# Where the encoder memory is split in a hybrid encoder step, and which engines square it

## The chip, the cores and the metric

One core of one Trainium2 chip. The time is device microseconds for one execution of the whole program; lower is better. The engines are TensorE (PE; its weight loads are listed apart as PEld), VectorE (DVE), ScalarE (ACT), GpSimd (POOL) and SyncE (SP), which issues the DMAs of the weights.

## The reference

One inference step of a two-layer streaming encoder with width 1024, for a prompt of 256 frames and a sample group of 32 frames that share the weights. Layer 0 has two attentions side by side, A (chunk-band attention with a position bias) and B (forgetting attention, whose bias is a running sum of log gates), eight heads of 64 each, with normalised queries and keys. Layer 1 has C (stick-breaking attention). Each layer then has cross-attention into 256 memory tokens, and an MLP with a squared ReLU. The parts that matter here:

```python
def rmsnorm(x, g):
    xf = x.astype(jnp.float32)
    y = xf * lax.rsqrt(jnp.mean(xf * xf, axis=-1, keepdims=True) + EPS)
    return (y * g.astype(jnp.float32)).astype(x.dtype)

def mem_kv(mem, g_mem, w_kv, k_gain):
    b, n, _ = mem.shape
    k, v = jnp.split(rmsnorm(mem, g_mem) @ w_kv, 2, axis=-1)
    k = rmsnorm(k.reshape(b, n, N_HEADS_X, HEAD_DIM_X), k_gain)
    return k, v.reshape(b, n, N_HEADS_X, HEAD_DIM_X)
```

The memory is the same in both layers, so the mean of its squares is computed once, in layer 0.

## The kernel before

All activations lie feature-major: 8 tiles of 128 features by 288 frames (256 + 32), the memory 8 tiles of 128 by 256. Products in full precision are three matmuls: every operand is split into a rounded high part and a low rest (`wh`, `wl` for weights, `xh`, `xl`, `mh`, `ml` and so on), and lines 159 to 161 (in `mm3`, called by `gemm`) multiply high by high, low by high and high by low. A projection of one chunk of 256 weight columns is two output tiles of 128 columns, eight feature tiles each, three matmuls, so 48 matmuls, into two of three PSUM banks (`ps_g`). Scaling by the factor of the input norm comes after the projection, when a bank is emptied: `t` (line 407) for queries and keys of A and B, `vT` (line 431) for values, `tmk` (line 353) for the memory's keys, which needs `memrs`, the factor from the memory's squares.

Weights stream in half chunks of four feature tiles (512 KB) through `load_chunk`: SP issues the load into one of four buffers of the ring `raw`, ACT rounds it to `wh` (line 144), and DVE, or every few times POOL, subtracts to get `wl` (line 145), in a ring of three half chunks.

The head norm (`headnorm`, `sum_parts`, called by `project_qk`) takes five buffers for each of two output tiles from the ring `f`, which has eight: `t`, its square `sqh`, the two parts `sh` and `sl` of that for a matmul against a block of ones, and the factor `r`.

`mem_split` loads the memory in two DMAs of 512 KB into the ring `raw` as well (`mraw`), makes `mh` on ACT and `ml` on DVE (tiles of the ring `sp`, which has four: `oh` and `ol` of the attention outputs take the others), and in layer 0 also the sum over the eight feature tiles of the squares: the first square goes directly into `mssum`, each of the seven others into a buffer `sqm` of the ring `f`, and is then added. `mem_rms` multiplies the sum by ones on PE and makes `memrs`.

The order of the program in layer 0 is written by hand in `ORD_AB`: `qA0` projects queries and keys of A's first four heads, `pA0` their values, `aA0` attends, `F` makes the forget gates, `M` is `mem_split`, `N` is `mem_rms` (its matmuls tied behind the last projection matmul traced before it), `K0` to `K3` project the memory's keys. A scheduler then lays out each engine's queue from this program order and the buffers that are free, so work of neighbouring steps is interleaved. B's attention needs its bias, which POOL builds at lines 845 and 846; the bias tiles `b1`, `b0` and `bsmp` have two buffers each.

Of the kernel before, what the change touches and what calls it, by code (L numbers as in the profile page):

```python
# [10 lines left out]
AF = mybir.ActivationFunctionType  # L11
ALU = mybir.AluOpType
# [3 lines left out]
NP_ = 256  # L16
# [13 lines left out]
HPG = 0  # L30
VT2 = 1
SHE = 0
ORD_AB = 'qA0 pA0 F qA1 pA1 aA0 M qB0 aA1 qB1 pB0 pB1 aB0 N K2 aB1 K0 K3 K1'.split()
ORD_C = 'M q0 q1 p0 a0 q2 p1 a1 q3 p2 a2 p3 a3 K0 K1 K2 K3'.split()
ORD_X = 's1 s2 s3 s0 v0 v1 S v2 v3'.split()
NWARM = 9
# [16 lines left out]
def body(ctx: ExitStack, tc: tile.TileContext, i: dict, o: dict):  # L53
    nc = tc.nc
    mm = nc.tensor.matmul
    dve = nc.vector
    act = nc.scalar.activation
# [237 lines left out]
    def mem_split(layer):  # L295
        mh = spp.tile([P, KT, T], F32R, tag="sp", name="mh")
        ml = spp.tile([P, KT, T], F32R, tag="sp", name="ml")
        if layer == 0:
            ssum = scr.tile([P, T], F32, tag="ssum", name="mssum", bufs=2)
        for k in range(KT):  # L300
            if k % 4 == 0:
                raw = wraw.tile([P, 4, NP_], F32, tag="raw", name="mraw")
                nc.sync.dma_start(out=raw, in_=i["memT"][:, k:k + 4, :])
            m = raw[:, k % 4, :]
            g = gT[:, 3, layer, k:k + 1]
            act(mh[:, k, 0:NP_], m, AF.Copy, scale=g)
            dve.scalar_tensor_tensor(ml[:, k, 0:NP_], m, g, mh[:, k, 0:NP_].bitcast(F32), ALU.mult, ALU.subtract)  # L307
            if layer == 0:
                if k == 0:
                    nc.gpsimd.tensor_tensor(ssum[:, 0:NP_], m, m, ALU.mult)  # L310
                else:
                    sq = scr.tile([P, T], F32, tag="f", bufs=FB, name="sqm")
                    nc.gpsimd.tensor_tensor(sq[:, 0:NP_], m, m, ALU.mult)
                    nc.gpsimd.tensor_tensor(ssum[:, 0:NP_], ssum[:, 0:NP_], sq[:, 0:NP_], ALU.add)
        return mh, ml, ssum if layer == 0 else None

    def mem_rms(ssum):
# [541 lines left out]
    qk, vs, mk0 = {}, {}, {}  # L859
    for step in ORD_AB:  # L860
        op, at = step[0], step[1:]
        kind, g = ("AB".index(at[0]), int(at[1])) if len(at) == 2 else (0, 0)
        if op == "q":
            qk[at] = project_ab(kind, g)
        elif op == "p":
            vs[at] = values_ab(kind, g)
        elif op == "a":
            group_ab(kind, g, *qk[at], vs[at])
        elif op == "F":
            forget()  # L870
        elif op == "M":
            mh, ml, msum = mem_split(0)
        elif op == "N":

            with tc.issue_after(last_mm[0].ins):
                mem_rms(msum)
        else:
            R.after = last_mm[0].ins if at == "0" else R.after
            mk0[int(at)] = mem_k(0, int(at), mh, ml)
# [15 lines left out]
    for step in ORD_C:  # L895
        op, g = step[0], int(step[1:] or 0)
        if op == "q":
            qk[g] = project_qk("sb_w", g, 4 + g, xh, xl, rs, None, "ckT", g)
        elif op == "p":
            vs[g] = project_v("sb_w", 8 + g, xh, xl, rs, "cvT", g)  # L900
        elif op == "a":
            attend_c(g, *qk[g], vs[g], *caches("cckT", "ccv", g), oh, ol)
        elif op == "M":
            mh, ml, _ = mem_split(1)
        else:
            mk1[g] = mem_k(1, g, mh, ml)
# [115 lines left out]
```

## Time and profile before

| | us |
|---|---|
| median of 3 runs (lowest to highest) | 976.09 (975.94 to 976.49) |
| the profiled execution | 975.05 |
| its span, first to last instruction | 973.4 |
| PE busy in the span | 956.0 |
| DVE busy | 682.8 |
| ACT busy | 542.8 |
| POOL busy | 251.4 |

The mean granted clock of TensorE is 0.996 of full speed. Layer 0's mixer, with the steps of `ORD_AB`, takes about the first 180 us, and the memory's split lies between 38 us (its loads) and 86 us. Rows of the profile name the engine, the line and the tiles, with buffer numbers left out; L144 is line 144 of the kernel. Times in the rows are microseconds from the start of the span; means are in nanoseconds.

### The profile page before, as it was taken

The page shows a single profiled execution, that of the slowest core. Times are in us where ns is not written, and L with a number is a line of the kernel's source. Part 1 is how long each engine was busy: PE and PEld are TensorE (multiplying, and loading weights), DVE is VectorE, ACT ScalarE, POOL GpSimd, SP SyncE. Part 2 cuts the span into 40 slices and gives each one's busy share as a digit, 9 for nine tenths or more (in the row PEclk, how much of TensorE's full clock was granted, in tenths as well). Part 3 has the DMA queues.
Part 4 walks back from the last instruction along what each step waited for, and adds up shares of the span by engine and source line. Part 5 has one row for each costly group of instructions (what it writes and reads, how often), then busy time and mean ns, then how long its engine had stood idle before and what let it go on. Part 6 is the DMA issues. An engine that isn't in the chain of part 4 may idle for free.

```text
span 973.4 us, 19368 instructions
## 1 busy us (share of the span) xinstructions
PE 956.0 (98%) x7276; PEld 922.0 (95%) x7276; DVE 682.8 (70%) x1460; ACT 542.8 (56%) x1268; POOL 251.4 (26%) x291
## 2 busy tenths in 40 slices
PE   8997999999999999999999999999999999999998
PEld 7996798899999999999999999989999999999998
DVE  7787777769778766777695666678987766564643
ACT  6665577555546644445474767765544555354531
POOL 5335322221112212121112332234443211111210
PEclk9998999999999999999999999999999999999999
DMA  8654343554455545555465444356444455555452
GB/s 264 235 171 140 132 166 118 197 185 154 153 172 174 168 159 170 164 164 169 158 214 193 134 150 146 118 174 207 152 145 136 154 173 166 162 167 169 162 172 73
DMA packets 50702, 160.03 MB, mean 164 GB/s; under 512 B 6296, under 2 KB 12968, under 8 KB 50352
## 3 DMA queue, kind: packets, MB, share of 16 engines
q1 hardware_dynamic: 46864, 148.69, 47.5%
q0 software_dynamic: 2592, 8.92, 2.4%
q10 hardware_dynamic: 1152, 1.18, 0.4%
q8 instruction: 57, 0.93, 0.4%
q14 instruction: 37, 0.30, 0.1%
HBM read 148.65 MB, written 10.12 MB: 163 GB/s over the span
## 4 chain that ended last, share of the span: by engine, by line
PE 95%; DVE 3%; DMA 1%; ACT 1%; issue 1%; SPq 0%; DVEq 0%
PE g L159 28%; PE g L161 27%; PE g L160 27%; PE po L474 1%; DVE wl L145 1%; PE za L474 1%; PE za L579 1%; PE s L517 1%; DVE ml L307 1%; DMA raw<-in_ab_w_dram 0%; PE zs L619 0%; DMA h<-in_xT_dram 0%; PE sx L159 0%; PE za L600 0%; PE sx L161 0%
## 5 line engine op out<-in xcount | busy, mean ns | idle before, releaser
L144 ACT ACTIVATE wh<-raw 128x512 fp32r<-128x512 f32 (+3 forms) x561 | 279.8, 550 | 235.2 <-PE g L160 117.9
L145 DVE TENSOR_TENSOR wl<-raw,wh 128x512 fp32r<-128x512 f32 (+3 forms) x483 | 307.9, 671 | 116.0 <-ACT wh L144 109.8
L145 POOL TENSOR_TENSOR wl<-raw,wh 128x512 fp32r<-128x512 f32 (+2 forms) x141 | 175.2, 1243 | 520.1 <-ACT wh L144 423.9
L159 PE MATMUL g<-xh,wh 128*128 128x288 f32 (+1 forms) x1032 | 302.9, 298 | 2.5 <-DVE t L407 1.5
L160 PE MATMUL g<-xl,wh 128*128 128x288 f32 (+1 forms) x1032 | 303.9, 297 | 1.0 <-DVE xl L197 1.0
L161 PE MATMUL g<-xh,wl 128*128 128x288 f32 (+1 forms) x1032 | 302.2, 297 | 1.3 <-DVE wl L145 1.3
L159 PEld LDWEIGHTS g<-xh,wh 128*128 128x128 f32 (+1 forms) x1032 | 192.3, 188 | 5.0 <-DVE t L407 2.1
L161 PEld LDWEIGHTS g<-xh,wl 128*128 128x128 f32 (+1 forms) x1032 | 192.8, 188 | 3.3 <-DVE wl L145 2.2
L160 PEld LDWEIGHTS g<-xl,wh 128*128 128x128 f32 (+1 forms) x1032 | 193.3, 188 | 2.7 <-DVE xl L197 1.7
L160 PE MATMUL g<-hl,wh 128*128 128x288 f32 x512 | 150.3, 295 | 0.0
L159 PE MATMUL g<-hh,wh 128*128 128x288 f32 x512 | 148.9, 295 | 0.0
L161 PE MATMUL g<-hh,wl 128*128 128x288 f32 x512 | 148.5, 294 | 0.0
L160 PEld LDWEIGHTS g<-hl,wh 128*128 128x128 f32 x512 | 96.1, 188 | 0.0
L161 PEld LDWEIGHTS g<-hh,wl 128*128 128x128 f32 x512 | 95.7, 188 | 0.0
L159 PEld LDWEIGHTS g<-hh,wh 128*128 128x128 f32 x512 | 95.3, 187 | 0.0
L160 PE MATMUL g<-ol,wh 128*128 128x288 f32 x256 | 75.1, 296 | 0.1
L159 PE MATMUL g<-oh,wh 128*128 128x288 f32 x256 | 73.9, 296 | 0.8 <-ACT oh L493 0.8
L161 PE MATMUL g<-oh,wl 128*128 128x288 f32 x256 | 73.5, 295 | 0.0
L775 DVE TENSOR_TENSOR h<-h,g 128x288 f32<-128x288 f32 x64 | 28.8, 450 | 29.6 <-PE g L161 29.5
L159 PEld LDWEIGHTS g<-oh,wh 128*128 128x128 f32 x256 | 47.4, 188 | 1.4 <-ACT oh L493 1.0
L160 PEld LDWEIGHTS g<-ol,wh 128*128 128x128 f32 x256 | 48.1, 188 | 0.3 <-DVE ol L494 0.3
L161 PEld LDWEIGHTS g<-oh,wl 128*128 128x128 f32 x256 | 47.6, 188 | 0.4 <-issue 0.4
(313 smaller groups left out, 1514.2 us busy)
## 6 DMA issues: line engine op xcount, KB each, us to landing
raw<-in_w_up_dram SPq DMA_DIRECT2D x64, 512.0 KB, 3.8
raw<-in_w_down_dram SPq DMA_DIRECT2D x64, 512.0 KB, 3.8
raw<-in_w_kv_dram SPq DMA_DIRECT2D x32, 512.0 KB, 3.8
raw<-in_sb_w_dram SPq DMA_DIRECT2D x24, 512.0 KB, 4.2
raw<-in_ab_w_dram SPq DMA_DIRECT2D x22, 512.0 KB, 4.4
raw<-in_w_q_dram SPq DMA_DIRECT2D x16, 512.0 KB, 4.2
raw<-in_w_o_dram SPq DMA_DIRECT2D x16, 512.0 KB, 4.0
raw<-in_ab_wo_dram SPq DMA_DIRECT2D x8, 512.0 KB, 3.8
```

What stands on the lines that cost most here:

```text
L144: act(wh[:, r, :], src, AF.Copy)
L145: e.tensor_tensor(wl[:, r, :], src, wh[:, r, :].bitcast(F32), ALU.subtract)
L159: mm(out, lh, rh, start=first, stop=False)
L160: mm(out, lh, rl, start=False, stop=False)
L161: return mm(out, ll, rh, start=False, stop=last)
L307: dve.scalar_tensor_tensor(ml[:, k, 0:NP_], m, g, mh[:, k, 0:NP_].bitcast(F32), ALU.mult, ALU.subtract)
L474: mm(po[64 * par:64 * par + 64, kk * P:NP_], vt[:, kk, cols], pts[par][kk], start=kk == 0, stop=kk == 1)
L517: mm(s[:, 0:NP_], q[:, P:NP_], kT[:, p, 0:NP_], start=True, stop=True)
L579: mm(za2, x[:, 0:P], y, start=f_, stop=False, skip_group_check=True)
L775: dve.tensor_tensor(h[:, kt, :], h[:, kt, :], ps[:, 0:T], ALU.add)
```

## The change

Two things. In `ORD_AB` the step `M` moves from behind `aA0`, ahead of `qB0`, to behind `qB1`, ahead of `pB0`. And the squares of the memory go from POOL to ACT, and the seven additions from POOL to DVE.

```diff
-ORD_AB = 'qA0 pA0 F qA1 pA1 aA0 M qB0 aA1 qB1 pB0 pB1 aB0 N K2 aB1 K0 K3 K1'.split()
+ORD_AB = 'qA0 pA0 F qA1 pA1 aA0 qB0 aA1 qB1 M pB0 pB1 aB0 N K2 aB1 K0 K3 K1'.split()
...
             if layer == 0:
                 if k == 0:
-                    nc.gpsimd.tensor_tensor(ssum[:, 0:NP_], m, m, ALU.mult)
+                    act(ssum[:, 0:NP_], m, AF.Square)
                 else:
                     sq = scr.tile([P, T], F32, tag="f", bufs=FB, name="sqm")
-                    nc.gpsimd.tensor_tensor(sq[:, 0:NP_], m, m, ALU.mult)
-                    nc.gpsimd.tensor_tensor(ssum[:, 0:NP_], ssum[:, 0:NP_], sq[:, 0:NP_], ALU.add)
+                    act(sq[:, 0:NP_], m, AF.Square)
+                    dve.tensor_tensor(ssum[:, 0:NP_], ssum[:, 0:NP_], sq[:, 0:NP_], ALU.add)
```

The title given to the change also names the sum tied behind the last projection and bias tiles twice; both stand in the kernel before already, and the diff does not touch them.

## The prediction

> **What bounds the kernel now.** I read the page first, then busy time by stretches, then what TensorE waited for, then the timelines of the one stretch that stands out.
>
> ```profile
> span 973.4 us, 19368 instructions
> PE 956.0 (98%) x7276; PEld 922.0 (95%) x7276; DVE 682.8 (70%) x1460; ACT 542.8 (56%) x1268; POOL 251.4 (26%) x291
> PE   8997999999999999999999999999999999999998
> PEclk9998999999999999999999999999999999999999
> PE 95%; DVE 3%; DMA 1%; ACT 1%; issue 1%; SPq 0%; DVEq 0%
> ```
>
> TensorE (PE) is the bound: 95% of the chain that ended last is its own work, and only 973.4 − 956.0 = 17.4 us of the span is idle. A change that touches no matmul can win only part of that, and of what a lowered clock costs. Both lie in one place, the fourth slice (73 to 97 us). By stretches (length; then busy time of PE, weight load, DVE, ACT, POOL, each with its count; granted clock, DMA share, GB/s):
>
> ```profile
> 30.00:75.00 45.00, 45.00 (x337) 42.34 (x336) 35.73 (x94) 29.14 (x77) 17.97 (x21) 1.00 0.57 181
> 75.00:90.20 15.20, 9.91 (x73) 7.18 (x73) 14.26 (x42) 9.74 (x27) 10.29 (x11) 0.92 0.51 159
> 90.20:140.00 49.80, 48.08 (x350) 43.65 (x349) 35.56 (x97) 30.58 (x84) 15.13 (x16) 0.96 0.40 133
> 180.00:190.00 10.00, 9.05 (x83) 8.35 (x82) 7.27 (x17) 6.80 (x17) 0.92 (x2) 1.00 0.68 235
> 190.00:973.00 783.00, 778.33 (x5970) 762.02 (x5969) 537.46 (x1066) 422.20 (x955) 186.01 (x199) 1.00 0.50 161
> ...
> 75.50:90.20 14.70, 0.34 (x2) 0.19 (x1) 0.92 0.52 161
> 90.20:94.60 4.40, 2.61 (x6) 1.99 (x6) 0.50 0.29 102
> ```
>
> Between 75.0 and 90.2 PE idles 15.20 − 9.91 = 5.29 us while DVE is busy 14.26 of 15.20: for these 15 us VectorE is the bound. The last two rows count line 160 alone, a third of each projection: two matmuls in 14.7 us, so PE lived on small attention products. Then, from 90.20 to 94.60, the clock is 0.50, which costs half of 4.40 = 2.2 us. The rest of the idle time is thin: 1.72 in 90 to 140, 0.95 in 180 to 190, 4.67 after that.
>
> Why the projections stood still shows in the timelines of DVE, ACT and POOL (start, length, engine, line, output<-input):
>
> ```profile
> 42.49 0.82 POOL L310 TENSOR_TENSOR mssum<-mraw 128x256 f32<-128x256 f32 x1
> ...
> 66.02 1.35 POOL L145 TENSOR_TENSOR wl<-raw,wh 128x512 fp32r<-128x512 f32 x1 [6.35 <-PE g L160]
> 66.10 0.50 ACT L183 ACTIVATE r<-ps_hn,epsb 128x288 f32<-128x288 f32 x1 [0.22 <-PE ps_hn L332]
> 67.33 4.71 POOL L313 TENSOR_TENSOR sqm<-mraw 128x256 f32<-128x256 f32 x6
> 68.18 0.44 DVE L407 TENSOR_TENSOR t<-g,rs 128x288 f32<-128x288 f32 x1
> 72.01 0.74 POOL L314 TENSOR_TENSOR mssum<-mssum,sqm 128x256 f32<-128x256 f32 x1
> 72.78 0.44 ACT L384 ACTIVATE sqh<-t 128x288 f32<-128x288 f32 x1 [1.67 <-POOL mssum L314]
> 74.97 0.38 ACT L488 ACTIVATE oh<-po 128x256 fp32r<-128x256 f32 x1 [0.71 <-PE po L474]
> 75.84 3.29 ACT L306 ACTIVATE mh<-mraw,gT 128x256 fp32r<-128x256 f32 x8
> 78.05 2.06 POOL L845 TENSOR_TENSOR b<-b,cq 128x1024 f32<-128x1024 f32 x1
> 78.28 2.00 DVE L328 CAST sh<-sqh 128x288 fp32r<-128x288 f32 x1
> 81.69 3.26 DVE L307 SCALAR_TENSOR_TENSOR ml<-mraw,gT,mh 128x256 fp32r<-128x256 f32 x4
> 82.04 3.48 POOL L314 TENSOR_TENSOR mssum<-mssum,sqm 128x256 f32<-128x256 f32 x4
> 89.36 0.45 DVE L407 TENSOR_TENSOR t<-g,rs 128x288 f32<-128x288 f32 x1
> ...
> PE s L517 <- DVE mx L458: 2.6, 2, 1.5
> PE g L159 <- DVE t L407: 1.5, 2, 0.9
> ```
>
> The seven squares `sqm` come from the ring `f` of eight buffers, which the head norm of B's queries (`t`, `sqh`, `sh`, `sl`, `r`) also uses. GpSimd starts six of them at 67.33, and the additions that free them run from 72.01 to 85.5, behind its own bias work (L845). So `sqh` of the first half waits for an addition (1.67 us), and `t` of the second half, which empties a projection bank, runs only at 89.36, 21 us after the first. With the banks full no projection can start. At the same time eight `ml` occupy DVE, slowed by the GpSimd work beside them (0.82 each in the four at 81.69).
>
> **The change, part by part.** The title's tie of the sum and the doubled bias tiles already stand in the kernel before (lines 875 and 832); the diff does not touch them, so they cost nothing.
>
> *M moves from before qB0 to behind qB1.* It takes with it 2 DMAs of 512 KB on SP's queue, 8 `mh`, 8 `ml` and the squares. I read the order of buffers from the rows: the squares start just after the previous norm's last new buffer (`r`, 66.10, then 67.33), although the first, which needs no buffer of that ring, ran at 42.49 and POOL had just idled 6.35 us; `mh` starts just after the first `oh` of its ring (74.97, then 75.84). So buffers are handed out in program order. Behind qB1, B's four head norms no longer queue behind squares. The gain if all of the stall goes: 5.29 + 2.2 = 7.5 us. The bound from the other side is 0: DVE stays the limit in that stretch because B's bias work on POOL (L845, L846) stays there.
>
> Cover for the gain: without M, DVE has 14.26 less 6.4 (the eight `ml`, below) = 7.9 us of work in 15.20, so it no longer fills the stretch even with POOL's bias work beside it.
>
> *SP's queue.* The two memory loads leave their place ahead of qB0's weights and go ahead of pB0's.
>
> ```profile
> 31.99 3.07 SPq L126 DMA_DIRECT2D raw<-in_ab_w_dram  x2
> 37.95 4.92 SPq L303 DMA_DIRECT2D mraw<-in_memT_dram  x2
> 45.54 6.85 SPq L126 DMA_DIRECT2D raw<-in_ab_w_dram  x3
> ```
>
> They hold two of the four `raw` buffers until the last square has read them: now 38 to about 86, then from 64 at the earliest (eight half chunks of 24 matmuls later, at the 337 matmuls in 45 us of the stretch 30 to 75, are 26 us) until B's last key norm. The weights of pB0, pB1 and K2 run through the other two, as those of qB0 do now; with two buffers PE was busy 45.00 of 45.00 from 30 to 75. Cost 0; if that cover were gone, a late half chunk is 24 matmuls or 3.2 us.
>
> *Squares and sums change engines.* Prices:
>
> ```profile
> L339 ACT ACTIVATE sqx<-tmk 128x256 f32<-128x256 f32 x16 | 6.3, 410 | 0.4 <-DVE tmk L353 0.4
> L340 DVE TENSOR_TENSOR sqx<-sqx 128x256 f32<-128x256 f32 x8 | 3.6, 445 | 2.2 <-ACT sqx L339 2.2
> L314 POOL TENSOR_TENSOR mssum<-mssum,sqm 128x256 f32<-128x256 f32 x7 | 5.5, 788 | 0.2
> L313 POOL TENSOR_TENSOR sqm<-mraw 128x256 f32<-128x256 f32 x7 | 5.3, 789 | 0.0
> L307 DVE SCALAR_TENSOR_TENSOR ml<-mraw,gT,mh 128x256 fp32r<-128x256 f32 x8 | 6.4, 826 | 0.6 <-ACT mh L306 0.6
> L307 DVE SCALAR_TENSOR_TENSOR ml<-mraw,gT,mh 128x256 fp32r<-128x256 f32 x8 | 3.6, 494 | 1.0 <-ACT mh L306 1.0
> ```
>
> The first `ml` row is the stretch 60 to 92, the second layer 1 (475 to 500), where no squares run on POOL. POOL loses 5.5 + 5.3 and one first square, some 11.6 us; ACT gains 8 × 0.41 = 3.3, DVE 7 × 0.445 = 3.1, and gets back up to 6.4 − 3.6 = 2.8 on `ml`. On DVE that is nearly even.
>
> *Where M lands.* `mh` and `ml` can start with their data, or behind the first `oh` (75) if that is later, and fill gaps. The squares must wait for the last `r` of B's keys, and two users wait behind them: K2's matmuls need `mh` and `ml` (early enough), and K2's evacuation `tmk` needs the sum.
>
> ```profile
> 134.07 0.48 ACT L183 ACTIVATE r<-ps_hn,epsb 128x288 f32<-128x288 f32 x1
> 136.79 0.38 PE L319 MATMUL ps_ms<-mssum,ones 128*128 128x256 f32 x1
> DVE tmk L353 <- ACT memrs L184: 0.7, 1, 0.7
> ```
>
> On today's clock: `r` at 134.07, seven squares in a row end 0.5 + 2.9 later at 137.5, the last additions at 138.4; today the sum is multiplied at 136.79, so `memrs` is 1.6 us later, and `tmk` already waits 0.7. Bounds: 0, if B's keys finish well ahead of pB1 (they no longer queue behind M), to 8.5 (rival 3). I take 1.5, by the row.
>
> Sum: −7.5 + 1.5 = −6.0. The profiled execution was 975.05 (span 973.4 plus 1.65 around it), so 969.05; it lies 1.04 below the median of the runs, 976.09. Against the median I forecast 970.1, its own range 968 to 972.3.
>
> **A rule weighed against a row.** The largest single idle piece of PE in the stretch, by the waits above, is 1.5 us, yet the clock halves at 90.2. The Trainium skill ("TensorE: Matmul & The Clock Gate", section "HAM oscillation — how this bites in real kernels") asks for no idle gap above about 3.4 us; by it, gaps of 1.5 us would not have lowered the clock, and the 2.2 us would not come back with this stall. The row speaks rather for the mean load: PE was busy 9.91 of 15.20 just before.
>
> **Rivals.**
> 1. *The stall goes, the low clock stays or recurs.* If the short idle pieces that remain in B's stage are enough, the 2.2 us stay: −5.29 + 1.5 = −3.8, 972.3. For it: `s` waits for `mx` would also come from aA1 and B's bias work. Against: in 30 to 75 the clock is 1.00 throughout. The page above would have it this way.
> 2. *The move only relocates the stall*, or B's bias on POOL was its cause. CAST `sh` took 2.00 us beside L845 (2.06), with no square involved. Then 7.5 comes back elsewhere: 976, no change. Against: `t` at 89.36 is held by buffers, and qB1's norm now has nobody in front.
> 3. *Slower: the sum comes late.* The squares sit behind the last `r`; DVE is busy 35.56 of 49.80 (71%) in 90 to 140, and if the seven additions only fill gaps (3.1 / 0.29 = 10.7 us), the last one ends near 145.3, and the sum is multiplied 8.5 us later. K2's two banks of three stay full, PE stops, and the clock drops again for 2.2: −7.5 + 8.5 + 2.2 = +3.2, 979.3. It decides from where the delay that PE sees passes 5.3 us. Against: PE has aB0's products as filler, and the squares precede pB0's work in program order.
>
> **How the numbers follow.** Chances: forecast 0.52, rival 1 0.17, rival 2 0.16, rival 3 0.15. A change within 0.2% (1.95 us) cannot be told from none. Faster: 0.52 + 0.17 and nothing of the others, 0.68 with a little off for mishaps; same 0.17; slower 0.15. The low end takes the whole 7.5 and the thin idle time of 90 to 140 (1.72), if B's earlier keys remove that too: 976.09 − 9.2 = 966.9. The high end reaches past rival 2 to 977.0, leaving out rival 3 and the tail, under 2 in 10.
>
> **What the profile after would show.** Right: no stretch of 15 us with two matmuls of L160 between 70 and 100; clock 1.00 there; second `t` of qB0 within 7 us of the first; no POOL `sqm`; `ml` near 0.5; `sqm` on ACT just after the last B-key `r`. Wrong: `tmk` waiting several us for `memrs` with PE idle behind it (rival 3); CAST still near 2 us and PE idle near 78 to 88 (rival 2); a clock of 0.5 somewhere in 70 to 140 with no stall of 5 us (rival 1). The plan of every later instruction is also drawn up anew; the 4.67 us idle after 190 could move by 1 us either way, inside the range.

## The result, and the profile after

| | before | changed |
|---|---|---|
| median of 5 executions, us (lowest to highest) | 975.94 (974.52 to 976.49) | 967.73 (965.68 to 970.41) |
| ratio, 95% interval | | 0.9926 (0.9903 to 0.9948) |
| profiled execution, us | 975.05 | 969.94 |
| its span, us | 973.4 | 968.2 |

The change is faster: 8.2 us by the medians, 7.2 us (5.1 to 9.5) by the ratio. 6.0 us were forecast, a time of 970.1 with its own range 968 to 972.3; the measured 967.73 lies just under that range, and inside the wide one of 966.9 to 977.0. The profiled execution of the changed kernel is one of its slower ones; two dips of the clock outside the changed stretch, told below, are in it.

Busy time by stretches of the changed kernel (length; PE, weight load, DVE, ACT, POOL with counts; granted clock, DMA share, GB/s), to be laid beside the rows of before:

```profile
30.00:75.00 45.00, 45.00 (x339) 42.68 (x337) 36.30 (x101) 30.11 (x79) 10.48 (x11) 1.00 0.58 178
75.00:90.00 15.00, 13.80 (x96) 11.46 (x96) 10.78 (x33) 9.19 (x26) 6.16 (x5) 1.00 0.37 119
90.00:100.00 10.00, 7.41 (x57) 6.16 (x57) 9.29 (x35) 6.95 (x22) 2.13 (x3) 0.85 0.35 113
100.00:140.00 40.00, 39.62 (x313) 36.23 (x312) 30.53 (x79) 25.01 (x69) 12.73 (x13) 1.00 0.52 169
92.00:96.00 4.00, 2.24 (x32) 1.67 (x32) 3.96 (x12) 3.83 (x12) 1.96 (x2) 1.00 0.26 85
96.00:100.50 4.50, 3.83 (x17) 3.74 (x17) 3.83 (x15) 1.81 (x6) 0.18 (x1) 0.62 0.58 188
```

From 75 to 90 PE now idles 1.20 us instead of 5.29, works 16 products of line 160 instead of 2, and the clock stays at 1.00. But a smaller stall stands right behind: 2.59 us idle in 90 to 100, and then 4.5 us at a clock of 0.62, some 1.7 us lost. Two other profiles of the changed kernel, taken with the experiments, have the same 2.59 and 2.61 us idle there. The timeline of DVE and ACT shows the head norm of B's queries freed, and where M's pieces came to lie:

```profile
66.76 0.46 DVE L407 TENSOR_TENSOR t<-g,rs 128x288 f32<-128x288 f32 x1
71.11 0.45 DVE L407 TENSOR_TENSOR t<-g,rs 128x288 f32<-128x288 f32 x1
77.79 0.42 ACT L310 ACTIVATE mssum<-mraw 128x256 f32<-128x256 f32 x1 [3.18 <-DMA mraw<-in_memT_dram]
78.75 1.70 ACT L306 ACTIVATE mh<-mraw,gT 128x256 fp32r<-128x256 f32 x4
84.91 0.43 DVE L407 TENSOR_TENSOR t<-g,rs 128x288 f32<-128x288 f32 x1
96.26 0.45 DVE L407 TENSOR_TENSOR t<-g,rs 128x288 f32<-128x288 f32 x1
130.71 0.48 ACT L183 ACTIVATE r<-ps_hn,epsb 128x288 f32<-128x288 f32 x1
131.09 1.94 ACT L313 ACTIVATE sqm<-mraw 128x256 f32<-128x256 f32 x6
139.24 0.76 DVE L353 TENSOR_TENSOR tmk<-g,memrs 128x256 f32<-128x256 f32 x2 [0.81 <-ACT memrs L184]
```

The two `t` of qB0 are 4.4 us apart (21 before). The squares start 0.4 us after the last `r` of B's keys. The pair of B's first keys, 84.91 and 96.26, is still 11 us apart: that is the stall that is left.

Two landmarks tell where the time was won: the first update of `h` by the mixer's output (line 651) and the first by the MLP behind it (line 775); the last start of line 775 is the last update of all. Before (first two rows) and changed (last two); the columns are count, shortest, median and longest in ns, first and last start:

```profile
L651 DVE TENSOR_TENSOR h<-h,g x32: 440/448/456, 184.4 to 765.1; 128x288 f32<-128x288 f32 x32
L775 DVE TENSOR_TENSOR h<-h,g x64: 439/452/455, 351.0 to 969.8; 128x288 f32<-128x288 f32 x64
...
L651 DVE TENSOR_TENSOR h<-h,g x32: 440/448/457, 177.8 to 760.0; 128x288 f32<-128x288 f32 x32
L775 DVE TENSOR_TENSOR h<-h,g x64: 440/452/456, 344.4 to 964.6; 128x288 f32<-128x288 f32 x64
```

Layer 0's mixer ends 6.6 us earlier (184.4 to 177.8), and the MLP behind the cross-attention starts as much earlier (351.0 to 344.4). In the two other profiles of the changed kernel that start is at 343.7 and 344.3, so 6.6 to 7.3 us are won by then, which agrees with the 7.2 of the ratio. Between the first and the last row of line 651 the changed execution loses 1.5 us again, in the same work: its clock is 0.97 in the 50 us from 643.4, where it was 1.00 before.

### The profile page after: what moved, and what is told of

It reads as the page before. It is cut to its first block, busy times and chain, and to the rows that moved or that the text cites. A ratio compares the mean times of both kernels' runs of the same rounds, so it can differ in the third digit from the quotient of the medians.

```text
span 968.2 us, 19370 instructions
## 1 busy us (share of the span) xinstructions
PE 954.6 (99%) x7276; PEld 923.8 (95%) x7276; DVE 682.0 (70%) x1467; ACT 543.0 (56%) x1276; POOL 236.9 (24%) x276
## 4 chain that ended last, share of the span: by engine, by line
PE 95%; DVE 2%; issue 1%; DMA 1%; POOL 1%; ACT 0%; SPq 0%; DVEq 0%; POOLq 0%
PE g L159 28%; PE g L161 28%; PE g L160 27%; PE za L474 1%; PE po L474 1%; PE za L579 1%; PE s L517 1%; PE zs L619 0%; DMA raw<-in_ab_w_dram 0%; PE sx L159 0%; PE sx L161 0%; PE ps_vt L434 0%; PE za L600 0%; PE sx L160 0%; PE xs L718 0%
## 5 line engine op out<-in xcount | busy, mean ns | idle before, releaser
L145 DVE TENSOR_TENSOR wl<-raw,wh 128x512 fp32r<-128x512 f32 (+3 forms) x483 | 309.7, 674 | 112.2 <-ACT wh L144 106.1
L145 POOL TENSOR_TENSOR wl<-raw,wh 128x512 fp32r<-128x512 f32 (+2 forms) x141 | 174.2, 1235 | 531.8 <-ACT wh L144 426.9
```

What stands on the lines that cost most here:

```text
L145: e.tensor_tensor(wl[:, r, :], src, wh[:, r, :].bitcast(F32), ALU.subtract)
```

## The experiments

Three causes were to be told apart: the ring (seven square buffers handed out ahead of B's query norm), the engine (GpSimd's work slowing VectorE), and the place (`mh` and `ml` in the way). Every kernel has its own runs of the kernel before on the same chip; ratios are against those.

**The order alone.** Squares and additions stay on GpSimd.

```diff
-ORD_AB = '... aA0 M qB0 aA1 qB1 pB0 ...'
+ORD_AB = '... aA0 qB0 aA1 qB1 M pB0 ...'
```

> Only the order changes: M behind qB1, squares and additions still on GpSimd. Ring theory (the seven square buffers stand ahead of B's query norm in the ring f): the stall of 7.5 us between 75 and 95 goes as in the full change, second t of qB0 within 7 us of the first; the squares and additions (about 10 us on GpSimd in a row) come behind the last r of B's keys near 131, so the sum is some 4 to 6 us later than in the changed kernel and part of the gain may be given back: 968 to 972 against 976. Port theory (GpSimd's squares slow VectorE, and taking them off GpSimd is the gain): the squares only move, so no more than 2 us gained, 974 or above.

969.65 us, ratio 0.9932 (0.9913 to 0.9950). The order alone brings nearly the whole gain (0.9926 for both parts), and the engine cause, called port theory above, falls: it allowed 2 us. The two `t` of qB0 are 4.4 us apart (66.26 and 70.61). The sum is late, as expected; its row, and PE around it:

```profile
L183 ACT ACTIVATE memrs<-ps_ms,epsb x1: 458/458/458, 146.0 to 146.0; 128x256 f32<-128x256 f32 x1
...
100.00:140.00 40.00, 39.57 (x309) 35.86 (x308) 28.83 (x76) 23.37 (x64) 19.86 (x25) 0.99 0.48 162
140.00:180.00 40.00, 39.21 (x328) 34.80 (x327) 31.89 (x90) 28.86 (x78) 10.42 (x11) 1.00 0.52 173
```

`memrs` at 146.0 is 8.6 us behind the 137.4 of the kernel before, just the delay of rival 3, and PE still works 39.57 and 39.21 of 40: it had other work, B's attention among it. The first update in the MLP comes at 345.4, against 343.7 to 344.4 in the changed kernel, so the later sum cost 1 to 2 us at most.

**The engines alone.** M stays ahead of qB0.

```diff
-nc.gpsimd.tensor_tensor(ssum[:, 0:NP_], m, m, ALU.mult)
+act(ssum[:, 0:NP_], m, AF.Square)
...
-nc.gpsimd.tensor_tensor(sq[:, 0:NP_], m, m, ALU.mult)
-nc.gpsimd.tensor_tensor(ssum[:, 0:NP_], ssum[:, 0:NP_], sq[:, 0:NP_], ALU.add)
+act(sq[:, 0:NP_], m, AF.Square)
+dve.tensor_tensor(ssum[:, 0:NP_], ssum[:, 0:NP_], sq[:, 0:NP_], ALU.add)
```

> Only the engines change: squares on ScalarE, additions on VectorE, M still before qB0. Ring theory: the buffers still stand ahead of B's query norm, but the squares take 2.9 us in a row and the additions 3.1, so the buffers come free near 72 to 75 instead of 85; half of the stall or less stays: 970 to 973, PE still idle 2 to 3 us in 75 to 90. Port theory: nearly all of the gain, 968 to 969, and ml at 0.5 us.

973.04 us, ratio 0.9972 (0.9961 to 0.9983), at the upper edge of what the ring theory gave, and far from the 968 to 969 of the port theory; PE idles 2.44 us in 75 to 90, as the ring theory had it. The last addition ends, and with it the ring is free, at 73.8 instead of 85.5, and the second `t` comes 10 us behind the first instead of 21:

```profile
70.36 0.45 DVE L407 TENSOR_TENSOR t<-g,rs 128x288 f32<-128x288 f32 x1
73.36 0.42 DVE L314 TENSOR_TENSOR mssum<-mssum,sqm 128x256 f32<-128x256 f32 x1
80.10 0.45 DVE L407 TENSOR_TENSOR t<-g,rs 128x288 f32<-128x288 f32 x1
```

**The ring alone.** The kernel before; only the buffer of the squares changes.

```diff
-sq = scr.tile([P, T], F32, tag="f", bufs=FB, name="sqm")
+sq = R.ph.tile([P, NP_], F32, tag="sqm", name="sqm", bufs=1)
```

> The kernel before with one line changed: sqm gets a ring of its own with one buffer, so that it stands ahead of nobody; order and engines as before (M before qB0, squares on GpSimd). Ring theory: squares run from about 43 when the memory lands, B's query norm is not held, second t of qB0 within 7 us of the first, most of the 7.5 us gained: 968 to 971. Port theory or position theory (eight mh and ml in the way at 76 to 86): stall stays, 974 to 976.

971.49 us, ratio 0.9951 (0.9934 to 0.9967): some 4.5 us from one line that changes neither order nor engines, a little short of the range. At the first update in the MLP (347.8 against 351.0) 3.2 us of it are to be seen, no more than with the engines alone (347.7). The squares, still on GpSimd and still in the old place, now start as soon as the memory has landed, and the two `t` are 4.3 us apart:

```profile
L313 POOL TENSOR_TENSOR sqm<-mraw x7: 616/711/952, 43.4 to 56.7; 128x256 f32<-128x256 f32 x7
...
68.80 0.45 DVE L407 TENSOR_TENSOR t<-g,rs 128x288 f32<-128x288 f32 x1
73.12 0.45 DVE L407 TENSOR_TENSOR t<-g,rs 128x288 f32<-128x288 f32 x1
...
90.00:100.00 10.00, 6.70 (x49) 5.85 (x50) 8.49 (x33) 6.59 (x20) 1.78 (x3) 0.76 0.43 146
...
79.59 2.51 DVE L307 SCALAR_TENSOR_TENSOR ml<-mraw,gT,mh 128x256 fp32r<-128x256 f32 x2
83.66 1.86 DVE L307 SCALAR_TENSOR_TENSOR ml<-mraw,gT,mh 128x256 fp32r<-128x256 f32 x3
```

The row of 90 to 100 shows that this kernel too has the second stall, 3.3 us idle. The last two rows, five of the eight `ml`, speak against the port theory once more: the eight take 0.90 us each on average, more than the 0.83 of the kernel before, and the time was won all the same. What the order brings beyond the ring, some 2 us (969.65 against 971.49, with intervals that overlap), is not told apart: `mh`, `ml` and the memory's loads move with M too.

**The ring of its own in the changed kernel.** The same line.

> The changed kernel with the same line: sqm in a ring of its own with one buffer. Ring theory: nothing is left to gain from the ring, the squares move from 131 to about 80 to 95, beside ml in the stretch where VectorE is fullest: 967 to 970, the same as the changed kernel within 2 us, or up to 2 us more. If the late sum at 131 to 139 cost something in the changed kernel: 1 to 2 us less, 966.

970.14 us, ratio 0.9937 (0.9922 to 0.9952), the same as the changed kernel. Behind qB1 the ring has nothing more to give. `memrs` starts at 133.7 here instead of 138.3, and that brings nothing back either; but the squares now lie in the crowded stretch (3.12 us idle in 90 to 100 instead of 2.59), which could hide a small gain.

**What is left: M's place.** M one step later, behind pB0, and two steps later, behind pB1; and the two memory loads alone back ahead of qB0.

```diff
-'... aA0 qB0 aA1 qB1 M pB0 pB1 aB0 ...'
+'... aA0 qB0 aA1 qB1 pB0 M pB1 aB0 ...'      first kernel
+'... aA0 qB0 aA1 qB1 pB0 pB1 M aB0 ...'      second
+'... aA0 L qB0 aA1 qB1 M pB0 pB1 aB0 ...'    third; L issues the two loads
```

> The changed kernel with M one step later, behind pB0: the memory loads stand behind pB0's weights, and mh and ml come some 10 to 15 us later, behind the stretch 78 to 91 in which A's second softmax and B's key norms want ScalarE and VectorE. Theory (what is left of the stall at 88 to 101 comes from mh and ml, and from ScalarE standing 5 us at the head of its queue for the memory loads): the idle time of 90 to 100 (2.6 us) and the low clock behind it (2 us) shrink: 2 to 4 us less than the changed kernel, 964 to 967. Rival (it comes from A's softmax chain and the ring f itself, five buffers for each norm): no change against the changed kernel, 967 to 970.

> M behind pB1, one more step later: mh and ml near 100 to 120, the second memory load late enough that K2's matmuls (from about 128) may wait for it. Theory (mh and ml in the way at 78 to 91): the same gain as behind pB0, 964 to 967, or part of it lost again to K2's start. Rival (softmax chain, ring): as the changed kernel, 967 to 970, or above where K2 waits.

> The changed kernel with the two memory loads alone back where M stood before (ahead of qB0), mh, ml, squares and additions behind qB1. ScalarE no longer stands for the loads at 74 to 78 and 84 to 86. If these waits (3.2 and 1.8 us) cost something: 1 to 3 us less than the changed kernel, 965 to 967. If ScalarE had nothing to do in them anyway: the same, 967 to 970; the loads then hold two of the four raw buffers 30 us longer, which should cost nothing.

> The changed kernel itself on the same chip as the three variants, so that they can be compared with it: 966 to 970.

971.55 (ratio 0.9956, 0.9940 to 0.9971), 970.80 (0.9952, 0.9939 to 0.9965) and 969.90 us (0.9944, 0.9932 to 0.9956), against 969.25 (0.9929, 0.9917 to 0.9941) for the changed kernel on the same chip. None is better, so my forecast of 964 to 967 from moving `mh` and `ml` away fails. The traces do not clear `mh` and `ml` altogether, because each new place brought a wait of its own. Behind pB0, SP issues the last two of the four loads of B's bias rows `bsmp` behind the first memory load, and two engines stand for DMAs that land near 88.5. `sl` of the head norm stands behind that wait in VectorE's queue, and PE waits 2.2 us for it (last row: idle time, count, longest):

```profile
88.94 0.19 DVE L854 SCALAR_TENSOR_TENSOR junk<-bsmp,eye 128x32 f32<-128x32 f32 x1 [4.87 <-DMA bsmp<-cd]
...
88.49 0.51 ACT L306 ACTIVATE mh<-mraw,gT 128x256 fp32r<-128x256 f32 x1 [4.94 <-DMA mraw<-in_memT_dram]
...
PE ps_hn L332 <- DVE sl L330: 2.2, 1, 2.2
```

Behind pB1, PE idles only 1.99 us in 75 to 100 (3.79 in the changed kernel), but 1.84 in 100 to 140 (0.38), where four `ml` take 5.34 us beside B's bias work on GpSimd, and PE waits 1.8 us for the `ol` behind them:

```profile
102.17 5.34 DVE L307 SCALAR_TENSOR_TENSOR ml<-mraw,gT,mh 128x256 fp32r<-128x256 f32 x4
PE po L474 <- DVE ol L489: 1.8, 1, 1.8
```

With the loads early, ACT's waits for them (3.2 and 1.8 us in the changed kernel) are gone, and PE still works only 7.46 of 10 us in 90 to 100, so taking these waits away brought nothing there:

```profile
90.00:100.00 10.00, 7.46 (x58) 6.03 (x57) 7.40 (x27) 4.98 (x17) 1.98 (x4) 0.83 0.59 184
```

**What is left: VectorE crowded.** In the changed kernel pB0 goes behind qB0, so that a projection without a head norm stands between; in a second kernel A's second attention goes behind qB1 instead.

```diff
-'... aA0 qB0 aA1 qB1 M pB0 pB1 aB0 ...'
+'... aA0 qB0 pB0 aA1 qB1 M pB1 aB0 ...'      first kernel
+'... aA0 qB0 qB1 aA1 M pB0 pB1 aB0 ...'      second
```

> The changed kernel with pB0 (the values of B's first four heads) moved from behind M to behind qB0. In the changed kernel PE still loses 2.6 us and then the clock near 88 to 101: A's second softmax fills VectorE, the second t of B's first keys runs 10.5 us after the first, and the three projection banks stay full. Theory (what is left is VectorE crowded by softmax and head norms together, with no projection that needs no norm in between): pB0 needs only one vT for each bank, so PE has work there: 2 to 4 us less than the changed kernel, 965 to 967. Rival (the banks are what is missing, whoever empties them, since vT stands in the same VectorE queue): the same as the changed kernel, 968 to 971.

> The changed kernel with A's second attention behind qB1 instead of before it, so that VectorE takes B's head norms first. Theory (crowded VectorE): the norms come without the softmax in between, the stall of 88 to 101 shrinks, but PE has less attention work to fill with, and the softmaxes of aA1 and aB0 come together near 110 to 130: between 965 and 972. Rival (banks and ring f): the four norms in a row go as fast as the eight buffers allow, 10 us for each pair, and PE idles more: 972 to 978.

> The changed kernel itself on the same chip, for comparison: 966 to 970.

With pB0 early 965.50 us, ratio 0.9894 (0.9881 to 0.9906), in the range of the theory; the changed kernel on the same chip 966.52, 0.9900 (0.9886 to 0.9914), so the gain over it is 1.0 us and not the 2 to 4 expected. With aA1 late 972.58, 0.9966 (0.9954 to 0.9979), between the ranges of the theory and its rival. There PE is busy without a break to 90, and then the scores `s` of A wait 2.9 us in one piece until VectorE has taken the maxima `mx` of those before; VectorE has no idle time from 86 to 96. The clock in 90 to 100 is 0.66 (releases of PE in that kernel: idle time, count, longest; then its stretch):

```profile
PE s L517 <- DVE mx L458: 2.9, 1, 2.9
...
90.00:100.00 10.00, 7.12 (x47) 5.85 (x45) 8.06 (x33) 4.65 (x18) 1.11 (x2) 0.66 0.45 133
```

The stretches of the kernel with pB0 early, the two `t` of B's first keys in it, and its landmark:

```profile
75.00:90.00 15.00, 14.73 (x101) 12.41 (x100) 9.86 (x28) 7.23 (x19) 6.73 (x5) 1.00 0.31 107
90.00:100.00 10.00, 9.33 (x87) 8.81 (x86) 9.06 (x30) 7.58 (x25) 2.39 (x3) 1.00 0.49 163
...
80.09 0.45 DVE L407 TENSOR_TENSOR t<-g,rs 128x288 f32<-128x288 f32 x1
90.30 0.45 DVE L407 TENSOR_TENSOR t<-g,rs 128x288 f32<-128x288 f32 x1
...
L651 DVE TENSOR_TENSOR h<-h,g x32: 440/449/456, 173.8 to 756.0; 128x288 f32<-128x288 f32 x32
```

The stall and the low clock are gone, PE idles 0.94 us in 75 to 100, and the mixer ends at 173.8, another 4 us earlier than in the changed kernel. The two `t` are still 10.2 us apart (11.4 in the changed kernel): the norm is hardly faster, but PE has pB0's products to do meanwhile. This kernel changes one thing more: the first memory load is issued at 81.8 instead of 70.6, and all eight `ml` run later, at some 0.48 us each, while GpSimd is idle. How much of the gain is due to that was not tried. Since the times on that chip did not separate the two kernels, a second set was taken.

> pB0 behind qB0 once more, for a second set of times beside the kernel before: the ratio of the changed kernel to the kernel before was 0.9926, 0.9929 and 0.9900 in three sets. If the missing stall and clock dip of 88 to 101 are worth their 4 us, the ratio is 0.987 to 0.990 again (964 to 966); if the first set was luck, 0.991 to 0.993 (967 to 969).

966.44 us, ratio 0.9895 (0.9875 to 0.9915): the same again. In three sets the changed kernel had 0.9926, 0.9929 and 0.9900, in two this one had 0.9894 and 0.9895. It is the fastest version here, about 2 us ahead of the changed kernel by these sets; on the one chip where both ran together their intervals overlap.

All versions together. The last column is the first update of `h` in the MLP, up to which every one of these profiles counts the same 2556 matmuls:

| kernel | median, us | ratio (95%) | MLP starts, us |
|---|---|---|---|
| before | 975.94 | 1 | 351.0 |
| changed | 967.73 | 0.9926 (0.9903 to 0.9948) | 344.4 |
| changed, beside the places of M | 969.25 | 0.9929 (0.9917 to 0.9941) | 343.7 |
| changed, beside pB0 early and aA1 late | 966.52 | 0.9900 (0.9886 to 0.9914) | 344.3 |
| order alone | 969.65 | 0.9932 (0.9913 to 0.9950) | 345.4 |
| engines alone | 973.04 | 0.9972 (0.9961 to 0.9983) | 347.7 |
| ring alone | 971.49 | 0.9951 (0.9934 to 0.9967) | 347.8 |
| changed, ring of its own | 970.14 | 0.9937 (0.9922 to 0.9952) | 344.7 |
| changed, M behind pB0 | 971.55 | 0.9956 (0.9940 to 0.9971) | 344.4 |
| changed, M behind pB1 | 970.80 | 0.9952 (0.9939 to 0.9965) | 345.3 |
| changed, loads early | 969.90 | 0.9944 (0.9932 to 0.9956) | 345.2 |
| changed, pB0 early | 965.50 | 0.9894 (0.9881 to 0.9906) | 340.4 |
| changed, pB0 early, again | 966.44 | 0.9895 (0.9875 to 0.9915) | 340.5 |
| changed, aA1 late | 972.58 | 0.9966 (0.9954 to 0.9979) | 347.7 |

## Why the prediction was right, point by point

- *Buffers are handed out in program order, and the squares stood in front of B's query norm.* Right, and shown to be a cause: one line that takes the squares out of the ring brings 4.5 us (3.2 at the start of the MLP). It is not the whole gain: the order alone, with GpSimd unchanged, brings 6.4 (969.65 against 976.04; 5.6 at the start of the MLP).
- *Gain 7.5 us if all of the stall goes.* The step that was mis-sized, and in two ways that nearly cancelled. The stall was worth more. I had read the clock as low only from 90.20 and priced that at 2.2 us, but it was 0.50 already in 88 to 90, and 0.76 on average in 85 to 90.2; with the 4.4 us behind that the low clock comes to some 3.4. PE's stretches before:

```profile
75.00:90.00 15.00, 9.71 (x72) 7.05 (x72) 14.06 (x41) 9.74 (x27) 10.29 (x11) 0.92 0.50 156
90.00:100.00 10.00, 9.82 (x59) 8.96 (x57) 6.57 (x26) 5.45 (x18) 0.49 (x2) 0.77 0.30 107
88.00:90.00 2.00, 1.67 (x25) 1.38 (x25) 2.00 (x12) 1.27 (x4) 0.00 (x0) 0.50 0.88 262
```

  With pB0 early, where nothing of the stall is left, the mixer ends 184.4 − 173.8 = 10.6 us earlier. Up to 8 of that lie in 75 to 100: the idle time falls from 5.47 to 0.94, and the low clock of some 3.4 is gone. Most of the rest is the thin idle time behind (1.54 in 100 to 140, and part of the 0.95 in 180 to 190). But not all of the stall goes with the change: the changed kernel keeps 2.59 us of idle time in 90 to 100 and 1.7 us of low clock. Its mixer ends 6.6 us earlier.
- *Late sum, 1.5 us.* Wrong: nothing, as far as the runs show. `memrs` starts 0.9 us later than before (138.3 against 137.4), `tmk` waits 0.81 us for it (0.7 before), and PE is busy 39.62 of 40 there. Squares behind the last `r`: right.
- *The sum, −6.0.* It came close partly by luck: the gain was taken 0.9 us too large (7.5 against 6.6), and a cost of 1.5 was added that did not come, which leaves 6.0 against 6.6 at the landmark.
- *Rival 3, the late sum makes it slower.* Its delay came in full in the kernel with the order alone (8.6 us) and cost 1 to 2 us at most. Its price left out the filler that I had named against it.
- *Rival 2, the stall only relocates.* True in small: a third or so of it stands again 10 us later, and at none of the places of M that were tried did it go. B's bias on POOL was not the cause of the whole: with the ring alone that work is still there. The kernels with pB0 early and with aA1 late point to VectorE filled by A's second softmax and B's norms at once, while PE has no projection whose bank can be emptied without a norm. That is argued and not singled out, since with pB0 early `mh` and `ml` move too.
- *Rival 1, the low clock recurs.* Also in small: its sign, a low clock without a stall of 5 us, is there in 96.0 to 100.5. Before it, the longest single idle piece of PE is 1.8 us:

```profile
PE ps_pt L523 <- ACT pt L527: 1.8, 1, 1.8
PE s L517 <- DVE mx L458: 1.1, 1, 1.1
```

  The gap of 3.4 us that the Trainium skill names ("TensorE: Matmul & The Clock Gate", section "HAM oscillation — how this bites in real kernels") was not needed here either: PE worked 2.24 of the 4.00 us from 92 to 96. Where no stall is left (pB0 early) the clock is 1.00 in both stretches.
- *DVE nearly even.* Not quite: `ml` takes 0.69 us in the changed kernel, not 0.49. No squares run on GpSimd there, but its other work does: two `ml` at 80.30 take 1.17 us each beside GpSimd's weight split (L145) and bias work (L846), and three at 89.30, while GpSimd is idle, 0.42 each.

```profile
80.30 2.33 DVE L307 SCALAR_TENSOR_TENSOR ml<-mraw,gT,mh 128x256 fp32r<-128x256 f32 x2
89.30 1.27 DVE L307 SCALAR_TENSOR_TENSOR ml<-mraw,gT,mh 128x256 fp32r<-128x256 f32 x3
...
79.68 1.46 POOL L145 TENSOR_TENSOR wl<-raw,wh 128x512 fp32r<-128x512 f32 x1
81.11 1.25 POOL L846 TENSOR_SCALAR_AFFINE_SELECT b<-b 128x1024 f32<-128x1024 f32 x1
92.79 1.70 POOL L145 TENSOR_TENSOR wl<-raw,wh 128x512 fp32r<-128x512 f32 x1 [10.44 <-ACT wh L144]
```

- *SP's queue at no cost.* Held in the changed kernel, as far as the kernel with the loads early shows (969.90 against 969.25 on the same chip). With M behind pB0, where part of `bsmp` is issued behind the memory load, PE waited 2.2 us behind VectorE's wait for `bsmp`; that the load held `bsmp` back is argued from the order of the queue.

## What to carry to other kernels

When an engine starves in a kernel whose buffers are handed out in program order, look for a side job whose temporaries share a ring with the critical chain: here a later place in the program was worth more (6.4 us) than a faster engine for it (3.0). A ring of its own is one line (4.5 us), but by the profiles it did not clearly beat the faster engine. Price a stall by where the next landmark lies in a kernel without it, not by idle time alone. And where a stall comes back one step later, try to put work between that needs little of the crowded engine.

## What the runs showed of the hardware that I had not expected

The clock falls to half for some 3 to 7 us near the start of the program in nine of the fourteen profiles: its mean in 5 to 20 us is 0.77 or 0.89 in these, and 1.00 in the other five. All three profiles of the changed kernel have it, the one of before does not.

```profile
10.00:20.00 10.00, 9.90 (x54) 9.16 (x54) 9.02 (x22) 7.17 (x19) 2.39 (x4) 0.75 0.88 295
...
10.00:20.00 10.00, 8.75 (x55) 7.42 (x54) 9.41 (x23) 8.12 (x20) 3.68 (x5) 1.00 0.88 299
```

(The first row is the changed kernel, the second the one before.) What it costs is not shown: of the changed kernel's profiles, one with 0.77 starts the MLP at 343.7, the one with 0.89 at 344.3. The mean clock of an execution goes roughly with its time: with the order alone, 966.60 us at 0.998 and 971.12 at 0.993, where 0.005 of 966 is 4.8 us. But the kernel before has 974.47 us at 0.992 and 976.81 at 0.996 on the same chip, so the clock is not all of it. Single executions of one kernel here lie up to 5.5 us apart (968.29 to 973.80 with M behind pB0), more than most of the differences that were to be told.
